# A causal convolution as banded matrices kept in DRAM, and one front part woven into a query part

## The chip, the core and the metric

The kernel runs on one core of a Trainium2 chip, as one program of about 54,000 instructions. The core has four engines that compute: TensorE (PE), VectorE (DVE), ScalarE (ACT) and GpSimd (POOL). SyncE (SP) issues most of the DMAs. Each engine works through its own instructions strictly in the order in which they were written into the program, and waits on semaphores for the others. The metric is the device time of one execution in microseconds.

## What is computed

One layer of a streaming encoder over 1024 tokens of width 1024. A shared projection feeds two groups, a convolution module and an RWKV-7 recurrence; their outputs are joined, projected, normalised, and sent through a PEER layer that picks 16 of 16,384 experts for each of 8 heads. The change touches the convolution module:

```python
u = p_conv[..., :CONV_WIDTH] * jax.nn.sigmoid(p_conv[..., CONV_WIDTH:])
u = lax.conv_general_dilated(
    u, conv_w[:, None, :], window_strides=(1,),
    padding=[(CONV_KSIZE - 1, 0)], dimension_numbers=('NWC', 'WIO', 'NWC'),
    feature_group_count=CONV_WIDTH) + conv_b
y_conv = jax.nn.silu(layer_norm(u, conv_ln_g, conv_ln_b))
...
x = layer_norm(ALPHA * x + gate1 * (jnp.concatenate([y_conv, y_rw], -1) @ w_out), ln1_g, ln1_b)
q = (adaln(x, shift2, scale2) @ peer_wq)
```

CONV_WIDTH is 512 channels and CONV_KSIZE 31 taps; each channel is convolved with its own taps over the tokens before it.

## The kernel before

The tokens are worked in two halves of 512. `inproj(h)` (from line 292) projects a half: it makes the inputs of the recurrence (r, k, v and what goes with them, stored to DRAM as AR_d, BK_d and v_d) and the gated input u of the convolution (`glu`). For half 0 this runs alone; for half 1 it is a generator whose steps are put between other work.

The recurrence is a scan over 16 chunks of 64 tokens. `solve(c)` builds and inverts a triangular system by a chain of short PE matmuls with DVE or POOL steps between them; `pass_state(c)` carries the state from chunk to chunk, and its first matmul (line 706) opens a chunk in PE's order. Solves run up to two chunks ahead. After every fourth chunk two token tiles of 128 are complete; `front(t0)` then projects 256 tokens with w_out and normalises them, and `query(t0)` multiplies them with peer_wq and sorts scores for the PEER layer. `choose` combines the sorted scores, and `gate_matrix` turns the choice into dense gate matrices, in stages of 32 tokens that are stored to G_d in DRAM. When all stages are there, the dense expert matmuls begin (lines 1294 and 1328). Three of the eight token tiles are gathered row by row instead, beside the dense part.

What sets the order: the scan's code calls `fill()` after its matmuls. Each call adds `rate[0]` to a credit; when it reaches RUN = 4, four steps of the list `side` are taken, which holds the second half's projection, then fronts and queries. Every fourth call takes one step of the list `slow`, which holds the convolution and the choices, and every twelfth one of `gates`. `RATES` gives the rate before and after chunk 3. At chunk 5 the second half's projection is finished by force, at chunk 9 the convolution, and the first entries of `firsts` (the first front and query). After the scan one loop empties the lists. A scheduler then places each instruction into its engine's order; the code's order is the priority, and it is not the final one.

`conv(h)` (from line 470) works the 512 channels as four tiles `ct` of 128 channels on partitions, 512 tokens in a row, with the 30 tokens before them in front (`ubuf`, `utail`). Of 31 taps DVE does 18, one multiply-add of 128x512 each (lines 479 and 484), in place. PE does 13 (PE_TAPS): ACT scales the identity by the tap's weights (line 490, a diagonal matrix), and PE multiplies it with the shifted window (line 492), float32 and 512 columns wide. DVE joins the two sums (line 495). Mean and variance over channels are matmuls with a matrix of ones (lines 498 and 506), and ACT, DVE and POOL finish the layer norm and the swish (lines 510 to 518), which stores conv_d for `front` to load.

A few lines say what a sentence can't:

```python
def fill():
    credit[0] += rate[0]
    fills[0] += 1
    if credit[0] >= RUN:
        credit[0] -= RUN
        for _ in range(RUN):
            step(side)
    if fills[0] % SLOW == 0:
        slow_step(1)
```

Of the kernel before, what the change touches and what calls it, by code (L numbers as in the profile page):

```python
# [10 lines left out]
F32 = mybir.dt.float32  # L11
# [22 lines left out]
HALF = 512  # L34
# [29 lines left out]
CD = 0  # L64
PIN = 3
STEPS = 4, 3
RATES = 1.0, 1.0
NPAGE = 30
TSLOW = 2
TGATE = 12  # L70
# [3 lines left out]
ABUF = 6  # L74
VBUF = 4

COLS = [("cond_b", 48), ("mu", 14), ("conv_w", 4 * KS), ("conv_b", 4), ("cln_g", 4), ("cln_b", 4),
        ("w0", 4), ("a0", 4), ("kk", 4), ("ka", 4), ("rk", 4), ("gn_g", 4), ("gn_b", 4)]
COFF = {}
_o = 0  # L80
for _n, _w in COLS:
    COFF[_n] = (_o, _o + _w)
    _o += _w
NCOLS = _o


@with_exitstack
def layer_kernel(ctx, tc, x, cols, c_row, cond_w, w_in, w2a2, g2, w_out, ln_rows, wq, keys, peer_u, peer_ut, peer_v, peer_vt, out):
# [7 lines left out]


    colt = const.tile([128, NCOLS], F32)
    ld(colt, cols)

    def col(n, i=None):
        a, b = COFF[n]
        return colt[:, a:b] if i is None else colt[:, a + i:a + i + 1]

    ident = const.tile([128, 128], F32)
# [46 lines left out]
    V.memset(ones_m, 1.0 / CW)  # L152
# [6 lines left out]
    def mm(w=512):  # L159
        return psum.tile([128, 512], F32, tag="mm", name="mm")[:, :w]  # L160
# [4 lines left out]
    def page(name, dt=F32, w=512):  # L165
        return pgp.tile([128, max(w, 512)], dt, tag="pg", name=name)[:, :w]
# [81 lines left out]
    def run(jobs):  # L248
        for j in jobs:
            yield from j  # L250

    def drain(gen):
        for _ in gen:
            pass
# [24 lines left out]
    ubuf = [fe.tile([128, 4, KS - 1 + HALF], F32, name="u", bufs=1) for _ in range(1)][0]  # L279
    utail = fe.tile([128, 4, KS - 1], F32)  # L280
    G.memset(utail, 0.0)
# [10 lines left out]
    def inproj(h, ps, pg_):  # L292
# [5 lines left out]
        def tp(name):  # L298
            return pg_.tile([128, 512], F32, tag="pg", name=name)
# [165 lines left out]

    def behind(h):
        return tc.issue_after(ready[h].ins) if h in ready else nullcontext()
    PE_TAPS = 13

    def conv(h):  # L470
        acc = []
        for ct in range(4):
            wk = lambda k: colt[:, COFF["conv_w"][0] + KS * ct + k:COFF["conv_w"][0] + KS * ct + k + 1]
            win = lambda k: ubuf[:, ct, k:k + HALF]
# [5 lines left out]
            i, j = 1, KS - PE_TAPS  # L480
            while i < KS - PE_TAPS or j < KS:
                for _ in range(3):
                    if i < KS - PE_TAPS:
                        V.scalar_tensor_tensor(a, win(i), wk(i), a, op0=OP.mult, op1=OP.add)
                        i += 1
                if j < KS:
                    n = min(2, KS - j)
                    dg = page("ctap").rearrange("p (k c) -> p k c", k=4)
                    for k in range(n):
                        A.activation(dg[:, k, :], ident, AF.Copy, scale=wk(j + k))  # L490
                    for k in range(n):
                        T.matmul(pt, dg[:, k, :], win(j + k), start=j + k == KS - PE_TAPS, stop=j + k == KS - 1)
                    j += n
                yield
            V.tensor_add(a, a, pt)
        pmn = mm()
        for ct in range(4):
            T.matmul(pmn, ones_m, acc[ct], start=ct == 0, stop=ct == 3)
        for ct in range(4):
            V.tensor_sub(acc[ct], acc[ct], pmn)  # L500
        yield
        pv = mm()
        for ct in range(4):
            s2 = page("s2")
            A.activation(s2, acc[ct], AF.Square)
            T.matmul(pv, ones_m, s2, start=ct == 0, stop=ct == 3)
        rs = page("crs")
        A.activation(rs, pv, AF.Sqrt, bias=eps_ln)
        V.reciprocal(rs, rs)
        yield  # L510
        for ct in range(4):
            y = acc[ct]
            V.tensor_mul(y, y, rs)
            A.activation(y, y, AF.Identity, bias=col("cln_b", ct), scale=col("cln_g", ct))
            sc_ = page("csig")
            A.activation(sc_, y, AF.Sigmoid)
            G.tensor_mul(y, y, sc_)
            ld(conv_d[h][ct], y)
            yield
        conv_left.remove(h)  # L520

# [267 lines left out]
    def front(t0, pg_):  # L789
# [3 lines left out]
        hp, hi = duo("ychi", F32R, pg_)  # L793
        lp, lo = duo("yclo", F32R, pg_)
        for i in range(KD // 2):
            f = pg_("ycf").rearrange("p (a t) -> p a t", a=2)
            if i < 2:
                c = t0 % HALF
                ld(f, conv_d[t0 // HALF][2 * i:2 * i + 2, :, c:c + n].rearrange("g p t -> p g t"))
# [4 lines left out]
            A.activation(hp[i], f, AF.Copy)  # L804
            G.tensor_sub(lp[i], f, hp[i].bitcast(F32))
        yield
        gate = [None, None]
        if (w_out.tensor.name, 0) not in split_d:
# [589 lines left out]
```

## Time and profile before

| what | value |
|---|---|
| median of three runs | 3205.79 us |
| lowest and highest | 3205.46 and 3208.14 us |
| the profiled execution | 3205.98 us |
| its span, first to last instruction | 3204.2 us |
| mean granted TensorE clock | 0.96 of full |
| convolution, first and last tap matmul, half 0 | 227.2 and 313.2 us from the span's start |
| first dense expert work without pause | about 1374.5 us |

Times in the profile are microseconds from the start of the span, unless marked ns. A group row gives a source line, engine, operation, the tiles written and read, and the count; then its busy time, the mean of one in ns, and the idle time of the engine ahead of it with what ended it. A float32 matmul leaves two records for each instruction. "x16" is a count of records. Matmuls overlap each other, so PE's busy time is not the sum of what each costs; the distance between neighbours is the cost of one.

### The profile page before, as it was taken

How to read it: one execution, taken by the hardware profiler on the slowest of the kernel's cores; microseconds unless marked ns; L12 is line 12 of the kernel's file. 1: busy time of each engine (PE TensorE's matmuls, PEld its weight loads, DVE VectorE, ACT ScalarE, POOL GpSimd, SP SyncE). 2: the span in 40 equal slices, each digit the busy share in tenths (PEclk: the TensorE clock that was granted, in tenths of full speed). 3: DMA queues.
4: the chain of work that ended last, by engine and by line, in shares of the span. 5: the costliest groups of instructions: out<-in, count | busy, mean ns of one | idle time of the engine just before them, and what ended most of it. 6: DMA issues, size and time to landing. Idle time of an engine off the chain costs nothing.

```text
span 3204.2 us, 53805 instructions
## 1 busy us (share of the span) xinstructions
PE 2993.7 (93%) x19952; PEld 2579.7 (81%) x19952; DVE 2513.0 (78%) x5677; ACT 1162.4 (36%) x2148; POOL 1761.6 (55%) x1368
## 2 busy tenths in 40 slices
PE   6969999899799888899999999999999999999995
PEld 4735676478678788889898898899999898999995
DVE  6379566867957899548999999988778777778788
ACT  5562444253434645643232232322223232222222
POOL 2410112143542433467777776777878778787872
PEclk9979998989789999999999999999999999999998
DMA  8876465378477998989999989899999989999994
GB/s 310 292 208 227 155 174 169 107 250 302 151 229 234 309 324 276 312 301 333 332 321 330 331 318 331 311 340 338 337 344 331 350 319 359 332 348 326 347 339 166
DMA packets 411783, 922.32 MB, mean 288 GB/s; under 512 B 81744, under 2 KB 221568, under 8 KB 389504
## 3 DMA queue, kind: packets, MB, share of 16 engines
q1 hardware_dynamic: 218688, 474.23, 43.1%
q0 software_dynamic: 110592, 402.70, 34.2%
q10 hardware_dynamic: 82240, 41.94, 4.7%
q8 instruction: 157, 2.57, 0.3%
q14 instruction: 106, 0.87, 0.1%
HBM read 788.91 MB, written 129.85 MB: 287 GB/s over the span
## 4 chain that ended last, share of the span: by engine, by line
PE 39%; DVE 12%; DMA 5%; issue 3%; POOL 1%; ACT 1%; SPq 0%; POOLq 0%; ACTq 0%; DVEq 0%
PE mg L1294 20%; PE md L1328 19%; DVE grow L1220 2%; DMA G_d<-stage 2%; DVE gy L1227 2%; DVE yacc L1333 1%; DMA grow<-peer_v,eid 1%; DMA vraw<-peer_vt 1%; POOL grow L1212 1%; DMA grow<-peer_u,eid 1%; POOL ulo L1255 1%; DVE mg L1298 0%; DVE ltkg L984 0%; DVE al L1300 0%; PE mgate L1058 0%
## 5 line engine op out<-in xcount | busy, mean ns | idle before, releaser
L1294 PE MATMUL mg<-h2h,uhi 128*128 128x320 f32 x2024 | 627.9, 310 | 12.6 <-DVE al L1300 9.5
L1294 PE MATMUL mg<-h2l,uhi 128*128 128x320 f32 x2024 | 626.3, 309 | 0.0
L1294 PE MATMUL mg<-h2h,ulo 128*128 128x320 f32 x2024 | 626.2, 310 | 0.0
L1227 DVE SCALAR_TENSOR_TENSOR gy<-grow,gz,gy 128x1024 f32<-128x1024 f32 x381 | 488.0, 1281 | 21.5 <-DMA grow<-peer_v,eid 17.3
L1328 PE MATMUL md<-vhi,al 128*128 128x512 f32 x1280 | 499.0, 391 | 0.0
L1328 PE MATMUL md<-vhi,ah 128*128 128x512 f32 x1280 | 493.1, 391 | 5.4 <-ACT ah L1299 3.8
L1328 PE MATMUL md<-vlo,ah 128*128 128x512 f32 x1280 | 497.3, 390 | 0.0
L1220 DVE SCALAR_TENSOR_TENSOR grow<-grow,gh 128x1024 f32<-128x1024 f32 x384 | 460.9, 1212 | 39.0 <-DMA grow<-peer_u,eid 35.7
L1212 POOL DMA_INDIRECT grow<-peer_u,eid x384 | 363.6, 947 | 192.3 <-DVE grow L1220 69.1
L1212 POOL DMA_INDIRECT grow<-peer_v,eid x384 | 362.8, 945 | 185.9 <-DVE gy L1227 83.8
L1294 PEld LDWEIGHTS mg<-h2h,uhi 128*128 128x128 f32 x2024 | 381.3, 188 | 21.7 <-DVE al L1300 13.3
L1294 PEld LDWEIGHTS mg<-h2l,uhi 128*128 128x128 f32 x2024 | 381.3, 188 | 4.8
L1294 PEld LDWEIGHTS mg<-h2h,ulo 128*128 128x128 f32 x2024 | 381.1, 188 | 2.8
L1255 POOL TENSOR_TENSOR ulo<-uraw,uhi 128x1024 fp32r<-128x1024 f32 x128 | 309.4, 2418 | 40.2 <-ACT uhi L1253 33.8
L1255 POOL TENSOR_TENSOR vlo<-vraw,vhi 128x1024 fp32r<-128x1024 f32 x128 | 309.3, 2416 | 24.6 <-ACT vhi L1253 20.1
L1333 DVE TENSOR_TENSOR yacc<-md,yacc 128x512 f32<-128x512 f32 x310 | 210.9, 685 | 110.9 <-PE md L1328 107.1
L1328 PEld LDWEIGHTS md<-vhi,ah 128*128 128x128 f32 x1280 | 240.1, 188 | 54.1 <-ACT ah L1299 5.3
L1054 POOL TENSOR_TENSOR ob<-mask,selt 128x384 f32<-128x384 bf16 x160 | 142.0, 899 | 256.2 <-PE mgate L1058 97.9
L1328 PEld LDWEIGHTS md<-vlo,ah 128*128 128x128 f32 x1280 | 240.6, 188 | 48.9
L1253 ACT ACTIVATE vhi<-vraw 128x1024 fp32r<-128x1024 f32 x128 | 135.2, 1056 | 398.7 <-DMA vraw<-peer_vt 369.4
L1328 PEld LDWEIGHTS md<-vhi,al 128*128 128x128 f32 x1280 | 240.5, 188 | 45.3 <-DVE al L1300 0.3
L186 POOL TENSOR_TENSOR wsplit<-wraw,wsplit 128x1024 fp32r<-128x1024 f32 x46 | 116.3, 2530 | 228.6 <-ACT wsplit L185 194.7
(405 smaller groups left out, 5764.0 us busy)
## 6 DMA issues: line engine op xcount, KB each, us to landing
uraw<-peer_ut SPq DMA_DIRECT2D x128, 512.0 KB
vraw<-peer_vt SPq DMA_DIRECT2D x128, 512.0 KB
wsplit<-split_wq SPq DMA_DIRECT2D x48, 1024.0 KB
G_d<-stage ACTq DMA_DIRECT2D x20, 2048.0 KB
gmat<-G_d SPq DMA_DIRECT2D x32, 1024.0 KB
cw<-cond_w SPq DMA_DIRECT2D x48, 512.0 KB
wsplit<-split_w_out SPq DMA_DIRECT2D x24, 1024.0 KB
split_w_in<-wsplit SPq DMA_DIRECT2D x22, 1024.0 KB
```

Source lines behind the costliest of these rows:

```text
L186: G.tensor_sub(lo, raw, hi.bitcast(F32))
L1054: G.tensor_mul(ob[:, :3], mb[:, :3], gt[:, c:c + 3, None].to_broadcast([128, 3, 128]))
L1212: G.indirect_dma_start(out=r, out_offset=None, in_=peer_u if k < 128 else peer_v, in_offset=bass.IndirectOffsetOnAxis(ap=eid[:, k % 128:k ...
L1220: V.scalar_tensor_tensor(r, r, 1.0, ht, op0=OP.mult, op1=OP.mult, accum_out=z[:, i:i + 1])
L1227: V.scalar_tensor_tensor(y, r, z[:, i - 128:i - 127], y, op0=OP.mult, op1=OP.add)
L1253: A.activation(hi, raw, AF.Copy)
L1255: G.tensor_sub(lo, raw, hi.bitcast(F32))
L1294: T.matmul(p, l[:, k, :], r[k][:, bs], start=i == 0, stop=i == 3 * KD - 1)
L1328: T.matmul(p, l[:, ts], r[:, e % 2, :], start=e == 0 and q == 0, stop=e == 3 and q == 2)
L1333: ins = V.tensor_add(ya, p, ya)
```

## The change

The convolution is laid out anew. A partition no longer holds one channel with 512 tokens in a row, but one of 32 channels and one of PH = 4 phases of the tokens (token number modulo 4). Four groups g of 32 channels fill a tile, each with 128 time steps of 4 tokens. Then one matrix of 128x128 per lag carries the taps from four phases to four phases, and LAGS = 9 lags cover 31 taps. A tile takes 4 x 9 = 36 matmuls of 128 columns, a half 144. No tap is done on DVE.

The matrices are banded: 32x32 blocks that are diagonal. For the first half POOL builds them, four to a page, as a product of a small identity (`eye32`) and the weights (line 512 of the new kernel), 36 pages in all, and stores each page to `tape_d` in DRAM (line 515). For the second half the pages are loaded back (line 510) instead. The weights come in a tile of their own, `convt`.

To bring u into phases, ACT's sigmoid and DVE's product in `glu` read PSUM with a step of four, u is stored to DRAM with four DMAs per tile, and `conv` loads it as (phase, channel) with the 8 steps before. Mean and variance use a matrix of ones in 32x32 blocks, over 16 pieces of 128 columns. The result is stored with four DMAs per tile, and `front` reads it back with two loads per page, so that ACT's and POOL's splitting steps there come in two pieces.

Beside it the order of the parts changes. At chunk 7 (MERGE) the new front, of tokens 256 to 511, is no longer put behind the first query: `beside` takes a step of each in turn, and the pair takes the query's place in `side` and in `firsts`, so that both are finished by force at chunk 9. The rate of side steps after chunk 3 falls from 1.0 to 0.5.

```diff
+MERGE = 7,
+CY = 2
+RELOAD = 1
-RATES = 1.0, 1.0
+RATES = 1.0, 0.5
+PH = 4
+LAGS = 9
...
-    conv_d = dt([4, 128, HALF], "conv_d", 2)
+    conv_d = dt([4, 128, PH, 128], "conv_d", 2)
+    tape_d = dt([LAGS, 128, 512], "tape_d", 4) if RELOAD else None
+    u_d = dt([4, PH, 32, S // PH], "u_d", 4)
...
-                s_ = tp("gsig")
-                A.activation(s_, pg, AF.Sigmoid)
-                A.activation(ubuf[:, ct, :KS - 1], utail[:, ct, :], AF.Copy)
-                V.tensor_mul(ubuf[:, ct, KS - 1:], pa, s_)
-                A.activation(utail[:, ct, :], ubuf[:, ct, HALF:], AF.Copy)
+                s_ = tp("gsig").rearrange("p (q t) -> p q t", q=PH)
+                A.activation(s_, pg.rearrange("p (t q) -> p q t", q=PH), AF.Sigmoid)
+                V.tensor_mul(s_, pa.rearrange("p (t q) -> p q t", q=PH), s_)
+                for g in range(4):
+                    ld(u_d[ct][g, :, :, 128 * h:128 * h + 128].rearrange("q c t -> c q t"), s_[32 * g:32 * g + 32])
...
+            ld(ubuf[ct][:, :, o:], u_d[ct].rearrange("g q c t -> (q c) g t")[:, :, 128 * h - LAGS + 1 + o:128 * h + 128])
+        yield
+        for ct in range(4):
             a, pt = page("cacc"), mm()
             acc.append(a)
-            with behind(0) if PIN & 1 else nullcontext():
-                V.tensor_scalar(a, win(0), wk(0), col("conv_b", ct), op0=OP.mult, op1=OP.add)
...
-                        V.scalar_tensor_tensor(a, win(i), wk(i), a, op0=OP.mult, op1=OP.add)
...
-                        A.activation(dg[:, k, :], ident, AF.Copy, scale=wk(j + k))
...
-                        T.matmul(pt, dg[:, k, :], win(j + k), start=j + k == KS - PE_TAPS, stop=j + k == KS - 1)
...
-            V.tensor_add(a, a, pt)
+            w = col("conv_w")[:, 4 * PH * LAGS * ct:4 * PH * LAGS * (ct + 1)]
+            for i in range(4 * LAGS // 4):
+                dg = page("ctap")
+                if h and RELOAD:
+                    ld(dg, tape_d[ct][i])
+                else:
+                    G.tensor_mul(dg.rearrange("p (j c) -> p j c", c=32), eye32[:, None, :].to_broadcast([128, 16, 32]),
+                                 w[:, 16 * i:16 * i + 16, None].to_broadcast([128, 16, 32]))
+                    if RELOAD:
+                        ld(tape_d[ct][i], dg)
+                for j in range(4):
+                    g, m = divmod(4 * i + j, LAGS)
+                    T.matmul(pt[:, 128 * g:128 * g + 128], dg[:, 128 * j:128 * j + 128],
+                             ubuf[ct][:, g, LAGS - 1 - m:LAGS - 1 - m + 128], start=m == 0, stop=m == LAGS - 1)
+                if i % CY == CY - 1:
+                    yield
+            V.tensor_tensor(four(a), four(pt), wide("conv_b", ct), op=OP.add)
+            yield
...
-            firsts.append(front(64 * (c - 3), page))
-            side.insert(0 if c in AHEADF else len(side), firsts[-1])
+            f_ = front(64 * (c - 3), page)
+            if c in MERGE and side:
+                m_ = beside(f_, side[-1])
+                firsts[:] = [m_ if f is side[-1] else f for f in firsts]
+                side[-1] = m_
+            elif c in AHEADF:
+                side.insert(0, f_)
+            else:
+                side.append(f_)
+            firsts.append(f_)
```

More of the change, by code (lines that the diff above doesn't have):

```diff
@@ L83 @@
     _o += _w
-NCOLS = _o
+NCOLS = COFF["conv_w"][0]
+NCONV = _o - NCOLS
 @with_exitstack
@@ L98, in layer_kernel @@
     colt = const.tile([128, NCOLS], F32)
-    ld(colt, cols)
+    ld(colt, cols[:, :NCOLS])
+    convt = []
     def col(n, i=None):
         a, b = COFF[n]
+        if a >= NCOLS:
+            a, b = a - NCOLS, b - NCOLS
+            return convt[0][:, a:b] if i is None else convt[0][:, a + i:a + i + 1]
         return colt[:, a:b] if i is None else colt[:, a + i:a + i + 1]
@@ L151, in layer_kernel @@
     ones_m = fe.tile([128, 128], F32)
-    V.memset(ones_m, 1.0 / CW)
+    V.memset(ones_m, 0.0)
+    for q in range(PH):
+        V.memset(ones_m[32 * q:32 * q + 32, 32 * q:32 * q + 32], 1.0 / CW)
+    eye32 = fe.tile([128, 32], F32, name="eye32")
+    V.tensor_reduce(eye32, ident.rearrange("p (q c) -> p c q", q=PH), axis=AX.X, op=OP.add)
     iota_q = const.tile([128, TOPK, TOPK], BF, name="iota_q")
@@ L250, in run, with beside @@
             yield from j
+    def beside(a, b):
+        a, b = [a], [b]
+        while a or b:
+            step(a)
+            step(b)
+            yield
     def drain(gen):
@@ L278, in layer_kernel @@
     V.memset(mask0.rearrange("p (c t) -> p c t", t=64)[:, :, 0:1], 0.0)
-    ubuf = [fe.tile([128, 4, KS - 1 + HALF], F32, name="u", bufs=1) for _ in range(1)][0]
-    utail = fe.tile([128, 4, KS - 1], F32)
-    G.memset(utail, 0.0)
+    ubuf = [fe.tile([128, 4, LAGS - 1 + 128], F32, name=f"u{ct}", bufs=1) for ct in range(4)]
+    for ct in range(4):
+        G.memset(ubuf[ct][:, :, 0:LAGS - 1], 0.0)
+    convt.append(fe.tile([128, NCONV], F32, name="convt"))
+    ld(convt[0], cols[:, NCOLS:])
     V.memset(last, 0.0)
@@ L467, in behind @@
         return tc.issue_after(ready[h].ins) if h in ready else nullcontext()
-    PE_TAPS = 13
     def conv(h):
+        four = lambda a: a.rearrange("p (g t) -> p g t", g=4)
+        wide = lambda n, ct: col(n)[:, 4 * ct:4 * ct + 4, None].to_broadcast([128, 4, 128])
         acc = []
         for ct in range(4):
-            wk = lambda k: colt[:, COFF["conv_w"][0] + KS * ct + k:COFF["conv_w"][0] + KS * ct + k + 1]
-            win = lambda k: ubuf[:, ct, k:k + HALF]
+            o = 0 if h else LAGS - 1
+            ld(ubuf[ct][:, :, o:], u_d[ct].rearrange("g q c t -> (q c) g t")[:, :, 128 * h - LAGS + 1 + o:128 * h + 128])
@@ L476, in conv @@
+        yield
+        for ct in range(4):
             a, pt = page("cacc"), mm()
             acc.append(a)
-            with behind(0) if PIN & 1 else nullcontext():
-                V.tensor_scalar(a, win(0), wk(0), col("conv_b", ct), op0=OP.mult, op1=OP.add)
[L480 to L494, printed above, removed]
@@ L497, in conv @@
+            V.tensor_tensor(four(a), four(pt), wide("conv_b", ct), op=OP.add)
+            yield
+        across = lambda a: a[:, None, :].to_broadcast([128, 4, 128])
+        pmn = mm(128)
+        for i in range(16):
+            T.matmul(pmn, ones_m, acc[i // 4][:, 128 * (i % 4):128 * (i % 4) + 128], start=i == 0, stop=i == 15)
         for ct in range(4):
-            T.matmul(pmn, ones_m, acc[ct], start=ct == 0, stop=ct == 3)
-        for ct in range(4):
-            V.tensor_sub(acc[ct], acc[ct], pmn)
+            V.tensor_sub(four(acc[ct]), four(acc[ct]), across(pmn))
@@ L501, in conv @@
         yield
-        pv = mm()
+        pv = mm(128)
         for ct in range(4):
@@ L505, in conv @@
             A.activation(s2, acc[ct], AF.Square)
-            T.matmul(pv, ones_m, s2, start=ct == 0, stop=ct == 3)
-        rs = page("crs")
+            for g in range(4):
+                T.matmul(pv, ones_m, s2[:, 128 * g:128 * g + 128], start=ct == g == 0, stop=ct == g == 3)
+        rs = page("crs", w=128)
         A.activation(rs, pv, AF.Sqrt, bias=eps_ln)
@@ L512, in conv @@
             y = acc[ct]
-            V.tensor_mul(y, y, rs)
-            A.activation(y, y, AF.Identity, bias=col("cln_b", ct), scale=col("cln_g", ct))
+            V.tensor_mul(four(y), four(y), across(rs))
+            for g in range(4):
+                yg = y[:, 128 * g:128 * g + 128]
+                A.activation(yg, yg, AF.Identity, bias=col("cln_b", 4 * ct + g), scale=col("cln_g", 4 * ct + g))
             sc_ = page("csig")
@@ L517, in conv @@
             G.tensor_mul(y, y, sc_)
-            ld(conv_d[h][ct], y)
+            for q in range(PH):
+                ld(conv_d[h][ct].rearrange("(g c) q t -> c q g t", c=32)[:, q], four(y)[32 * q:32 * q + 32])
             yield
@@ L795, in front @@
         for i in range(KD // 2):
-            f = pg_("ycf").rearrange("p (a t) -> p a t", a=2)
+            f, h_, l_ = pg_("ycf").rearrange("p (a t) -> p a t", a=2), hp[i], lp[i]
             if i < 2:
-                c = t0 % HALF
-                ld(f, conv_d[t0 // HALF][2 * i:2 * i + 2, :, c:c + n].rearrange("g p t -> p g t"))
+                c = t0 % HALF // PH
+                f = f.rearrange("p a (q t) -> p a q t", q=PH)
+                h_, l_ = (z.rearrange("p a (t q) -> p a q t", q=PH) for z in (h_, l_))
+                for a in range(2):
+                    ld(f[:, a], conv_d[t0 // HALF][2 * i + a, :, :, c:c + n // PH])
             else:
@@ L803, in front @@
                        rwkv_d[tile0 + t][2 * i - 4:2 * i - 2].rearrange("g p t -> p g t"))
-            A.activation(hp[i], f, AF.Copy)
-            G.tensor_sub(lp[i], f, hp[i].bitcast(F32))
+            for a in range(2) if i < 2 else (slice(0, 2),):
+                A.activation(h_[:, a], f[:, a], AF.Copy)
+                G.tensor_sub(l_[:, a], f[:, a], h_[:, a].bitcast(F32))
         yield
```

21 lines of the change are left out of this document (9 added, 12 removed).

## The prediction

> **What bounds the kernel now.** I read the head of the page first, then the busy time of each engine by stage, then the groups of instructions, then the chain of waits.
>
> ```profile
> span 3204.2 us, 53805 instructions
> PE 2993.7 (93%) x19952; PEld 2579.7 (81%) x19952; DVE 2513.0 (78%) x5677; ACT 1162.4 (36%) x2148; POOL 1761.6 (55%) x1368
> ```
>
> The profiled execution took 3205.98 us, its span is 3204.2, and the median of the runs is 3205.79. I add to and take from 3206.0. A PE that is busy for 93% is an average over stages, so here are the stages. The columns are the stretch, its length, then PE, PE weight load, DVE, ACT and POOL busy with instruction counts, the granted clock, DMA share and GB/s.
>
> ```profile
> 0.00:213.00 213.00, 163.42 (x631) 117.66 (x631) 110.77 (x221) 119.29 (x207) 63.62 (x37) 0.90 0.80 277
> 213.00:254.50 41.50, 35.20 (x107) 19.48 (x104) 37.77 (x81) 16.28 (x40) 2.53 (x2) 0.92 0.77 217
> 254.50:368.50 114.00, 104.75 (x767) 67.40 (x766) 94.73 (x192) 41.56 (x99) 8.12 (x7) 0.91 0.59 197
> 368.50:534.50 166.00, 162.93 (x1655) 118.50 (x1653) 93.73 (x180) 72.89 (x134) 19.04 (x14) 0.98 0.54 157
> 534.50:665.50 131.00, 117.95 (x901) 72.35 (x899) 109.32 (x164) 52.10 (x116) 42.27 (x21) 0.91 0.48 159
> 665.50:827.50 162.00, 153.13 (x1768) 131.05 (x1764) 114.36 (x515) 62.41 (x130) 62.24 (x35) 0.92 0.83 286
> 827.50:999.50 172.00, 150.72 (x1627) 124.31 (x1628) 125.87 (x342) 75.18 (x158) 80.20 (x84) 0.81 0.57 182
> 999.50:1327.00 327.50, 287.60 (x2292) 273.15 (x2292) 285.99 (x1251) 170.00 (x350) 114.56 (x118) 0.97 0.88 297
> 1374.50:3204.20 1829.70, 1777.19 (x9939) 1617.14 (x9937) 1516.31 (x2684) 516.25 (x850) 1344.77 (x1024) 0.99 0.90 326
> ```
>
> I put the borders where the first state matmul of a chunk of the scan starts. Of that matmul's line alone, the same view counts 16 records for each chunk, which shows which chunks lie in a stage: 0 from 254.5, 1 to 4, 5 and 6, and 7 to 10 from 665.5.
>
> ```profile
> 254.50:368.50 114.00, 1.00 (x16) 0.72 (x16) 0.91 0.59 197
> 534.50:665.50 131.00, 1.34 (x32) 1.09 (x32) 0.91 0.48 159
> 665.50:827.50 162.00, 2.90 (x64) 2.27 (x64) 0.92 0.83 286
> ```
>
> The last stretch, the dense experts, is 1829.7 us with PE busy for 97%. The change adds and removes nothing there, so I carry it over unchanged. All that can move lies before 1374.5. Two stages there have DVE nearly full with the convolution, and these are its groups (busy us, mean ns):
>
> ```profile
> L484 DVE SCALAR_TENSOR_TENSOR cacc<-u,colt,cacc 128x512 f32<-128x512 f32 x136 | 109.7, 834 | 0.3
> L492 PE MATMUL mm<-u,ctap 128*128 128x512 f32 x208 | 101.0, 627 | 0.2 <-DVE xt L827 0.2
> L490 ACT ACTIVATE ctap<-ident,colt 128x128 f32<-128x128 f32 x104 | 33.7, 390 | 20.4 <-PE mm L492 16.8 <-DVE fa L581 2.3 <-DVE ia L575 1.0
> L495 DVE TENSOR_TENSOR cacc<-cacc,mm 128x512 f32<-128x512 f32 x8 | 5.4, 679 | 0.8 <-PE mm L492 0.8
> ```
>
> By the stage view of that DVE line alone, 14.1 + 35.5 = 49.6 us of the 109.7 lie in 213 to 368.5, and 60.1 in 534.5 to 665.5:
>
> ```profile
> 213.00:254.50 41.50, 14.09 (x20) 0.92 0.77 217
> 254.50:368.50 114.00, 35.53 (x49) 0.91 0.59 197
> 534.50:665.50 131.00, 60.09 (x68) 0.91 0.48 159
> ```
>
> So from 213 to 368.5 DVE works 132.5 of 155.5 us, and the scan's short matmuls, whose results DVE must mask and copy, stand in line behind taps.
>
> **The change, part by part.** PE first. A tap over 512 columns is two records; one of 128 columns also, and the gate matrices are such matmuls already.
>
> ```profile
> 264.09 2.84 PE L492 MATMUL mm<-u,ctap 128*128 128x512 f32 x6
> 886.88 1.06 PE L1058 MATMUL mgate<-oa,ob 128*128 128x128 f32 x8
> ```
>
> Taking one record's own 0.63 us off, six old ones come every (2.84 - 0.63) / 5 = 0.44 us; 52 matmuls of one half are 104 x 0.44 = 46 us. Eight narrow ones come every (1.06 - 0.29) / 7 = 0.11 us (0.29 is the mean of that line); the new half has 144 matmuls, 288 x 0.11 = 32 us. PE saves 14 us per half. The column means count as many columns as before. DVE loses 68 taps per half and keeps one addition per tile at L495's price. ACT loses 52 tap copies.
>
> POOL gets 36 tape products of 128x512 in the first half. No row has both inputs broadcast; the nearest of that shape are these:
>
> ```profile
> L517 POOL TENSOR_TENSOR cacc<-cacc,csig 128x512 f32<-128x512 f32 x8 | 10.7, 1357 | 24.0 <-ACT csig L516 24.0
> L430 POOL TENSOR_TENSOR a<-a,nr 128x512 f32<-128x512 f32 x8 | 12.6, 1572 | 139.9 <-DVE nr L425 96.0 <-issue 27.1 <-DVE rstd L216 16.8
> L1054 POOL TENSOR_TENSOR ob<-mask,selt 128x384 f32<-128x384 bf16 x160 | 142.0, 899 | 256.2 <-PE mgate L1058 97.9 <-DVE mask L1047 85.2 <-ACT oa L1053 43.7
> ```
>
> I take 1.36; the low end is 0.90 x 512/384 = 1.20, the high end 1.57, and twice the first for an access pattern that no row shows. POOL's order before, at the start of the scan (a, xm and MT are POOL's products of the mixing and of the solve):
>
> ```order
> L442 TENSOR_TENSOR xm<-xm,W 128x512
> L430 TENSOR_TENSOR a<-a,nr 128x512
> L442 TENSOR_TENSOR xm<-xm,W 128x512
> L640 TENSOR_TENSOR MT<-MT,eye_1458 128x256 x3
> L517 TENSOR_TENSOR cacc<-cacc,csig 128x512 x4
> ```
>
> and now:
>
> ```order
> L468 TENSOR_TENSOR xm<-xm,W 128x512
> L512 TENSOR_TENSOR ctap<-eye_168,convt 128x512 x9
> L456 TENSOR_TENSOR a<-a,nr 128x512
> L468 TENSOR_TENSOR xm<-xm,W 128x512
> L512 TENSOR_TENSOR ctap<-eye_168,convt 128x512 x20
> L673 TENSOR_TENSOR MT<-MT,eye_1487 128x256
> L512 TENSOR_TENSOR ctap<-eye_168,convt 128x512 x7
> L673 TENSOR_TENSOR MT<-MT,eye_1487 128x256 x2
> ```
>
> Twenty-nine tapes now stand ahead of the first solve's MT, and 36 ahead of the second's. PE, in the same place (arl is the scan's input, u the convolution's):
>
> ```order
> L518 MATMUL mm<-u_187,ctap 128x128 x5
> L665 MATMUL bank_1480<-arl,bkl 128x128 x4
> L518 MATMUL mm<-u_187,ctap 128x128 x14
> L665 MATMUL bank_1480<-arl,bkl 128x128 x4
> L518 MATMUL mm<-u_187,ctap 128x128 x9
> L739 MATMUL bank_1479<-SN,arl 64x64 x6
> ```
>
> So chunk 0's matmuls wait for 27 tapes, and POOL is the new pace-maker. It is free from 209.11 + 1.27 = 210.4 (first row below), so the last tape is there at 210.4 + 36 x 1.36 + 2 x 1.4 = 262. Before, PE issued its last tap at 313.2 (second row).
>
> ```profile
> 209.11 1.27 POOL L442 TENSOR_TENSOR xm<-xm,W 128x512 f32<-128x512 f32 x1 [2.86 <-DVE sq L438]
> L492 PE MATMUL mm<-u,ctap x104: 590/592/1220, 227.2 to 313.2; 128*128 128x512 f32 x104
> L620 SPq DMA_DIRECT2D arl<-AR_d x16: 359/377/939, 232.6 to 850.4; - x16
> 260.21 0.39 PE L198 MATMUL mm<-hlo,wsplit 128*128 128x512 f32 x1
> 260.44 0.62 PE L198 MATMUL mm<-hhi,wsplit 128*128 128x512 f32 x2
> ```
>
> Behind the last tap 55 us passed until chunk 1. That part now holds 28 more input matmuls, 6 us at 0.23 each (two in a row take 0.62, one 0.39, in the last two rows), so chunk 1 comes at 262 + 3 + 61 = 326 instead of 369: 43 us. SP's queue takes three off: the 36 tape stores and the u transfers stand ahead of loads that the scan needs, each with 0.38 us to issue (the third row); the loads of chunk 0, at 232.6 before, wait for tape 18 at 238. **First half: -40**, between -55 (1.20, no stall) and 0 (double price).
>
> Second half, 534.5 to 665.5: DVE falls from 109 to about 50 us and PE from 118 to 104, and both stop being full together. The tapes come back by 36 loads of 256 KB, 9.4 MB, 33 us at the 286 GB/s that the next stage reaches; DMA was busy for 0.48 x 131 = 63 us, so 96 in all fit beside PE's 104. PE then decides: 105 us. **Second half: -26**, between -35 and 0 (loads that stand behind the wraw waits in SP's order).
>
> The merge and the rate. In the stage of chunks 7 to 10 the same 384 query and 96 front matmuls are issued as before, but later: PE's order behind chunk 8's first state matmuls was
>
> ```order
> L706 MATMUL bank_1450<-SN,arl 64x64 x8
> L198 MATMUL mm<-h2hi,wsplit 128x256 x2
> L198 MATMUL mm<-h2lo,wsplit 128x256
> L198 MATMUL mm<-h2hi,wsplit 128x256 x2
> L198 MATMUL mm<-h2lo,wsplit 128x256
> ```
>
> and is now
>
> ```order
> L739 MATMUL bank_1479<-SN,arl 64x64 x8
> L678 MATMUL bank_1480<-eye_1487,vl 64x64
> L679 MATMUL bank_1480<-eye_1487,vl 64x64
> L678 MATMUL bank_1480<-eye_1487,vl 64x64
> L679 MATMUL bank_1480<-eye_1487,vl 64x64
> ```
>
> Chunks 7 and 8 run bare, and query and front crowd into 9 and 10. A chunk cost no less than 31 us even where PE was not full:
>
> ```profile
> 902.00:933.50 31.50, 1.39 (x16) 1.01 (x16) 0.84 0.83 265
> 968.50:999.20 30.70, 0.68 (x16) 0.54 (x16) 0.91 0.80 252
> ```
>
> Then 32 MB (16 raw tiles of 0.5 MB, 16 stores of 1 MB, 8 reloads of 1 MB) at 286 / 0.83 = 345 GB/s take 93 us, 115 at 277 GB/s. 62 + 110 - 162 = **+10**, between -7 and +30.
>
> After the scan 584 instead of 520 gate matmuls remain, but 984 instead of 1056 of the query. Sixteen more groups of four cost DVE a mask and a product each, 0.68 + 0.28 us, 15 us; 6 fewer score matmuls mean 6 fewer sorts of five steps like L784's, 0.28 x 5 x 6 = 8 us less. DVE is busy for 286 of 327.5 us there: **+7**, 0 to 20.
>
> ```profile
> L1047 DVE TENSOR_TENSOR mask<-iota_b,selbank 128x1024 bf16<-128x1024 bf16 x128 | 86.1, 678 | 19.8 <-POOL ob L1054 11.0 <-ACT oa L1053 6.0 <-ACT selt L1027 1.6
> L1055 DVE TENSOR_TENSOR ob<-mask,selbank 128x128 f32<-128x128 bf16 x128 | 33.5, 279 | 35.4 <-PE mgate L1058 30.3 <-POOL ob L1054 2.4
> L784 DVE FIND_INDEX8 vi<-vi,s 128x8 uint32<-128x128 f32 x96 | 26.6, 284 | 0.0
> ```
>
> Before 213, 16 u stores and ACT and DVE reading every fourth column: **+2**, 0 to 8 (16 issues at 0.38 us, if nothing hides them).
>
> The sum: 3206 - 40 - 26 + 10 + 7 + 2 = **3159 us**.
>
> [...]
>
> **The rivals.**
>
> *POOL's tapes cost double.* With 2.7 us each the last is there at 311, as late as the last tap was: the first term is gone, 3199. For it: POOL's rows scatter, and no row has two broadcasts. Against: L1054 broadcasts one input at no visible cost.
>
> *Half the clock in the bare chunks.* Eight gate matmul records took 2.07 us in a stretch with PE idle, 1.06 later:
>
> ```profile
> 862.83 2.07 PE L1058 MATMUL mgate<-oa,ob 128*128 128x128 f32 x8
> ```
>
> If chunks 7 and 8, whose PE work by the order is about 20 us, run so, they take 20 us more: 3179. Against: a chunk waits mostly for DVE. [...]
>
> *The gate stages end the front, and begin later: slower.* The chain of waits passes through the stores of the gate stages:
>
> ```profile
> 1340.71 15.39 DMA G_d<-stage
> L1066 ACTq DMA_DIRECT2D G_d<-stage x20: 366/366/400, 902.5 to 1375.5; - x20
> ```
>
> Nineteen steps took 473 us. The first stage stood behind chunk 11 in PE's order, now behind chunk 14. With my terms chunk 15 begins at 999 - 54 = 945 and the first stage ends near 925, against 902.5. If the steps keep their 24.9 us, the dense part starts 22 us later, whatever was saved: 3228. It decides if a stage can't come faster than that; but the last ones came 10 to 15 us apart, since the store above was the wait.
>
> *Nothing lost in the merge.* Without the third and fourth term, and with the first two at -48 and -33: 3127.
>
> **How the numbers follow.** Forecast 0.57, double tapes 0.12, half clock 0.13, gate stages 0.10, nothing lost 0.08. The range from 3120 to 3199 leaves out the gate stages, half the double tapes and little of the edges, about 2 in 10. A measurement here can tell 0.2%, 6.4 us, from no change. Faster: 0.55 of the forecast, 0.13, 0.08 and half of the tapes, 0.07, sum 0.83; same 0.07; slower 0.10.
>
> **What would show it.** Chunk 1's first state matmul near 328, the tapes' mean at 1.2 to 1.6 us, chunk 7's near 602, chunk 11's near 774, chunk 15's near 945, dense from about 1328. The forecast is wrong if the tapes are dearer, if tape loads arrive after PE wants them, if chunks 9 and 10 take over 130 us, or if the dense part isn't 1830 us long.

## The result and the profile after

The changed kernel takes 3174.0 us (median of four runs, 3168.5 to 3174.9) against 3205.6 of the kernel before: a ratio of 0.990, with a 95% interval from 0.9877 to 0.9922, so 25 to 39 us faster. A second series gave 3173.1 us and 0.9906 (0.9888 to 0.9925). The profiled execution took 3173.26 us, 32.7 less than the one of before.

The head of the page of the changed kernel:

```profile
span 3171.5 us, 54882 instructions
PE 2968.4 (94%) x20416; PEld 2622.4 (83%) x20416; DVE 2415.8 (76%) x5538; ACT 1133.7 (36%) x2058; POOL 1809.2 (57%) x1415
```

DVE lost 97 us of work and POOL gained 48, PE's busy time fell by 25. Now the stages, with the columns of the prediction's table (length, PE, weight load, DVE, ACT, POOL, clock, DMA share, GB/s). The borders are again the first state matmuls of chunks, here of 0, 1, 2, 5, 7, 11 and 15.

```profile
213.00:265.70 52.70, 49.67 (x316) 42.88 (x314) 39.62 (x82) 14.76 (x28) 36.05 (x31) 0.96 0.88 277
265.70:339.20 73.50, 72.18 (x788) 59.14 (x787) 46.00 (x93) 29.43 (x68) 17.61 (x15) 0.98 0.83 289
339.20:396.80 57.60, 53.86 (x471) 37.19 (x471) 41.89 (x83) 22.54 (x42) 4.23 (x3) 0.88 0.73 238
396.80:521.00 124.20, 119.13 (x1244) 88.35 (x1242) 67.39 (x126) 51.57 (x94) 16.03 (x13) 0.96 0.57 162
521.00:625.00 104.00, 99.10 (x1070) 86.25 (x1068) 44.81 (x83) 36.89 (x70) 34.44 (x20) 0.95 0.80 278
625.00:801.00 176.00, 158.56 (x1790) 138.65 (x1786) 100.15 (x396) 66.92 (x137) 59.83 (x36) 0.83 0.79 270
801.00:957.50 156.50, 136.41 (x1527) 116.32 (x1527) 133.28 (x502) 60.87 (x135) 71.66 (x73) 0.84 0.60 198
```

Chunk 1 to chunk 2, the third row, is 57.6 us long (58.4 by the two starts). Before it was 42.5 with PE never idle:

```profile
368.50:411.00 42.50, 42.50 (x435) 30.13 (x434) 24.67 (x46) 18.79 (x37) 4.59 (x3) 1.00 0.59 172
```

In the ledger below, "mark" is the hundredth matmul record of the line that opens the dense part (L1294 before, L1331 now), a clearer border than the first record. All of it is read off the starts of those records, in us; "second profile" is another profile of the changed kernel (after_again below).

| stretch | before | after | difference | second profile | forecast |
|---|---|---|---|---|---|
| 213 to chunk 2 | 198.5 | 183.9 | -14.6 | -17.2 | -40 |
| chunks 2 to 4 | 123.8 | 123.7 | -0.1 | -1.7 | 0 |
| chunks 5, 6 | 130.5 | 104.0 | -26.5 | -26.6 | -26 |
| chunks 7 to 10 | 162.1 | 176.4 | +14.3 | +13.5 | +10 |
| chunk 11 to the mark | 561.2 | 555.6 | -5.6 | -12.2 | +7 |
| behind the mark | 1815.1 | 1814.9 | -0.2 | +0.4 | 0 |

Two profiles of the same kernel lie up to 12 us apart at the mark (1356.6 and 1344.9), but only 3 at chunk 2. So I read causes from the stages, and a whole time only from its interval.

One row is 25 us short of its forecast, the first half's. The page's own chain of waits names a suspect that stands in no term of the prediction, a DMA of `cond_w`:

```profile
PE mg L1331 22%; PE md L1365 21%; PE mm L214 5%; PE mm L860 2%; PE mgate L1095 2%; DMA cw<-cond_w 2%; DVE grow L1257 2%; DVE gy L1264 2%; PE mm L518 1%; DVE mask L1084 1%; DVE yacc L1370 1%; DMA G_d<-stage 1%; PE bank L697 1%; PE bank L723 1%; POOL grow L1249 1%
```

These are the columns of the modulation that come from the condition vector: `cond_some` loads a 512 KB tile and DVE multiplies it with the vector and sums. 16 of 48 are done at the start, 32 beside the scan's first chunks. They share two buffers with the raw weights (WRAW = 2). By tile, the changed kernel and then the kernel before:

```profile
L291 SPq DMA_DIRECT2D cw<-cond_w x48: 327/328/1687, 8.8 to 361.7; - x48
L293 DVE SCALAR_TENSOR_TENSOR cw<-cw,silc x48: 1182/1224/3427, 17.5 to 370.1; 128x1024 f32<-128x1024 f32 x48
  DMA cw<-cond_w: 21.8, 18
```

```profile
L267 SPq DMA_DIRECT2D cw<-cond_w x48: 327/328/990, 8.3 to 329.3; - x48
L269 DVE SCALAR_TENSOR_TENSOR cw<-cw,silc x48: 1211/1218/3395, 17.6 to 333.6; 128x1024 f32<-128x1024 f32 x48
  DMA cw<-cond_w: 4.8, 10
```

The last line of each is DVE's idle time until such a load (us, times). The products are the same, but DVE waits 21.8 us instead of 4.8, and the last product starts at 370, well behind chunk 1 (339), where before it started at 334, ahead of chunk 1 (369). Between chunk 1 and chunk 2 alone, the stage view of this tile counts 22 records of DVE, 11 products with their read-outs, 13.6 us of work, and the waits there for its loads are 12.7 us; before, none of the products lay in this stretch:

```profile
338.50:396.90 58.40, 13.55 (x22) 0.88 0.74 239
DVE cw L293 <- DMA cw<-cond_w: 12.7, 9, 5.3
```

### The profile page after: what moved, and what is told of

It reads as the page before. It is cut to its first block, busy times and chain, and to the rows that moved or that the text cites. A ratio compares the mean times of both kernels' runs of the same rounds, so it can differ in the third digit from the quotient of the medians.

```text
span 3171.5 us, 54882 instructions
## 1 busy us (share of the span) xinstructions
PE 2968.4 (94%) x20416; PEld 2622.4 (83%) x20416; DVE 2415.8 (76%) x5538; ACT 1133.7 (36%) x2058; POOL 1809.2 (57%) x1415
## 4 chain that ended last, share of the span: by engine, by line
PE 59%; DVE 19%; DMA 6%; issue 4%; POOL 2%; ACT 2%; SPq 0%; POOLq 0%; ACTq 0%; DVEq 0%
PE mg L1331 22%; PE md L1365 21%; PE mm L214 5%; PE mm L860 2%; PE mgate L1095 2%; DMA cw<-cond_w 2%; DVE grow L1257 2%; DVE gy L1264 2%; PE mm L518 1%; DVE mask L1084 1%; DVE yacc L1370 1%; DMA G_d<-stage 1%; PE bank L697 1%; PE bank L723 1%; POOL grow L1249 1%
## 5 line engine op out<-in xcount | busy, mean ns | idle before, releaser
L1331 PE MATMUL mg<-h2h,uhi 128*128 128x320 f32 x2024 | 626.9, 310 | 7.8 <-DVE al L1337 7.7
L1331 PE MATMUL mg<-h2l,uhi 128*128 128x320 f32 x2024 | 625.8, 309 | 0.0
L1331 PE MATMUL mg<-h2h,ulo 128*128 128x320 f32 x2024 | 625.4, 309 | 0.0
L1331 PEld LDWEIGHTS mg<-h2h,uhi 128*128 128x128 f32 x2024 | 380.5, 188 | 16.9 <-DVE al L1337 12.0
L1331 PEld LDWEIGHTS mg<-h2l,uhi 128*128 128x128 f32 x2024 | 380.4, 188 | 5.3
L1331 PEld LDWEIGHTS mg<-h2h,ulo 128*128 128x128 f32 x2024 | 380.3, 188 | 2.8
L214 PE MATMUL mm<-hhi,wsplit 128*128 128x512 f32 x672 | 227.6, 412 | 8.7 <-ACT gsig L389 5.4
```

Of the source, the lines that this page charges most:

```text
L214: T.matmul(pt, l[:, k, :], r[k], start=i == 0, stop=i == 3 * KD - 1)
L1331: T.matmul(p, l[:, k, :], r[k][:, bs], start=i == 0, stop=i == 3 * KD - 1)
```

## The experiments

**The theories.** T: the taps were the cover of this chain. With two buffers a tile can't be loaded before the one two places ahead has been multiplied; while it was on its way DVE had taps to do. Without taps DVE stands at the product, in order, and the solves' steps stand behind the wait and the products. S: the 36 tape stores, on SP's queue and as holders of POOL's pages, ate the gain. A: the merge and the slower rate ate it.

The start of the first state matmul of some chunks, in us, and the mark, for all that was profiled:

| kernel | 0 | 1 | 2 | 5 | 7 | 11 | 15 | mark |
|---|---|---|---|---|---|---|---|---|
| before | 255 | 369 | 411 | 535 | 666 | 828 | 999 | 1389 |
| after | 266 | 339 | 397 | 521 | 625 | 801 | 957 | 1357 |
| after_again | 268 | 341 | 394 | 516 | 620 | 796 | 950 | 1345 |
| conv_only | 268 | 340 | 395 | 518 | 623 | 788 | 977 | 1369 |
| no_rate | 266 | 339 | 394 | 516 | 621 | 785 | 975 | 1373 |
| rebuild | 251 | 356 | 404 | 521 | 629 | 809 | 960 | 1368 |
| wraw4 | 268 | 341 | 382 | 511 | 612 | 797 | 959 | 1350 |
| before_wraw4 | 258 | 382 | 422 | 553 | 694 | 864 | 1010 | 1409 |
| after_nocond | 264 | 339 | 378 | 509 | 615 | 792 | 939 | 1336 |
| late_tapes | 249 | 354 | 396 | 522 | 623 | 808 | 955 | 1347 |
| wraw4_act | 278 | 349 | 391 | 520 | 625 | 812 | 973 | 1365 |
| conv_wraw4 | 267 | 340 | 380 | 511 | 610 | 799 | 964 | 1337 |
| conv_wraw4_b | 267 | 339 | 380 | 508 | 608 | 792 | 954 | 1328 |
| conv_wraw4_late | 249 | 357 | 395 | 526 | 636 | 811 | 972 | 1345 |

Each edit also lets the scheduler place other instructions anew, so a row differs by more than its edit.

**1. The parts of the change.** First the convolution without merge and rate, then with the merge alone.

```diff
-MERGE = 7,
+MERGE = ()
-RATES = 1.0, 0.5
+RATES = 1.0, 1.0
```

> The changed kernel with MERGE empty and RATES back to 1.0, 1.0: the convolution's part alone. Read off the two traces, that part brought chunk 2 forward by 14.5 us and the stage of chunks 5 and 6 by 27 us, and the stage of chunks 7 to 10 became 14 us longer. Theory A (the merge and the slower rate cost what they were priced at, 10 + 7 us): stage of chunks 7 to 10 back at 162 us, the dense part begins some 10 to 17 us earlier than with the whole change, time 3157 to 3165 us. Rival B (that stage is longer because everything ahead of it came earlier, so its 32 MB of transfers decide, whatever the order): stage at 170 to 176 us, time 3170 to 3178. Rival C (merge and rate pay later, by taking gate work out of the scan): time 3180 or more.

```diff
-RATES = 1.0, 0.5
+RATES = 1.0, 1.0
```

> The changed kernel with RATES back to 1.0, 1.0 and the merge kept. Theory A (the slow rate leaves chunks 8 and 9 bare, at a granted clock of 0.65 and 0.50, and crowds 10 and 11): the clock between chunk 7 and chunk 9 comes back over 0.8, the stage of chunks 7 to 10 falls from 176 to some 162 us, time 3160 to 3167. Rival B (transfers decide that stage): stage within 4 us of 176, time 3170 to 3178.

> The changed kernel itself once more, beside the others on one chip. The whole change against the convolution alone (3181.8 us, 0.9914): theory C (merge and slower rate together repay some 8 us after the scan): 0.9885 to 0.9900, chunk starts within 4 us of the first profile. Rival A (they cost 10 us or more, and the first measurement was a lucky chip): 0.993 or more.

Measured: conv_only 3181.8 us, 0.9914 (0.9897 to 0.9930); no_rate 3185.2, 0.9933 (0.9915 to 0.9951); the whole change once more 0.9906 (0.9888 to 0.9925), its profile within 3 us of the first up to chunk 2, and 12 ahead at the mark. A falls as the cause: without merge and rate the time is not shorter. For conv_only that is what rival C forecast; no_rate came out longer than either theory had it, and after_again between its two. In its stage A was right about the length: chunks 7 to 10 take 165 us in conv_only and 164 in no_rate, and 176 with the slower rate (the clock between chunk 7 and chunk 9 did not come back over 0.8 in no_rate, it was 0.76). But conv_only needs 580 us from chunk 11 to the mark, the whole change 556 and 549. Merge and rate together are worth 0.0008 to 0.0015 of the time, which these intervals can't tell from nothing; the slow rate by itself, 0.9933 against 0.9906 and 0.9899, gains 9 to 11 us by the ratios, with intervals that overlap. What the convolution brings is nearly all of the result.

**2. Tapes built twice, none stored.**

```diff
-RELOAD = 1
+RELOAD = 0
```

> The changed kernel with RELOAD = 0: no tape is stored or loaded, POOL builds all 36 again in the second half. Theory S (the tape stores held the first half up: POOL waited 8.0 us for them, and SP's queue carries 36 of them): chunk 0's first state matmul at 257 instead of 265.7, chunk 2's at 386 to 389 instead of 397, the second half's stage at 104 to 108 us since POOL has room for 38 us more there, time 3162 to 3168. Rival T (what is missing in the first half is the chain of condition products, each waiting for its load): chunk 0 some 8 us earlier, but chunk 2 at 395 to 397, time 3172 to 3178. Rival U (the second half's gain needs the loads): its stage at 115 us or more, time over 3180.

Measured: 3185.0 us, 0.9928 (0.9916 to 0.9941). S's forecast failed: two of chunk 0's 16 matmuls started at 251, the rest at 269, and chunks 1 and 2 came later than with the stores (356 and 404). DVE's waits for condition tiles were 28.2 us there. The last tape of the first half ended at 279 us, against 277 with the stores, so doing without the stores did not bring the tapes earlier; why chunk 1 was 18 us later all the same stays open. The second half needs no loads: 629 - 521 = 108 us, against 104. T's number for chunk 2 (395 to 397) and its time (3172 to 3178) were missed too.

**3. Four buffers for the condition's tiles**, in the changed kernel and in the kernel before.

```diff
-WRAW = 2
+WRAW = 4
```

> The changed kernel with four buffers instead of two for the raw weights, which the 32 condition products between chunks 0 and 2 share. Theory T (with the taps gone nothing covers the load of each condition tile; DVE waited 21.8 us for them, SP 26 us for DVE to free a buffer): DVE's waits on these loads fall under 6 us, chunk 2's first state matmul comes at 382 to 388 instead of 397, time 3159 to 3166. Rival S (the tape stores are what holds the first half up): waits fall too, but chunk 2 stays at 394 to 397, time 3170 to 3176.

> The kernel before with four raw buffers instead of two. Theory T (before, DVE's taps covered the loads of the condition tiles: DVE waited 4.8 us for them in all): chunk 2's first state matmul within 4 us of 411.5, time within 5 us of the kernel before, ratio 0.998 to 1.002. Rival G (four buffers help any version of this kernel, through the projections' raw weights): 10 us or more faster, ratio under 0.997, seen before 213 us or in chunks 7 to 10.

Measured: wraw4 3161.5 us, 0.9858 (0.9843 to 0.9874); before_wraw4 3218.8, 1.0049 (1.0030 to 1.0067). DVE's waits for condition tiles in wraw4, by the tile view:

```profile
  DMA cw<-cond_w: 10.0, 4
```

and the stretch from chunk 1 to chunk 2 there, by the stage view, then what is left of this chain in it (records of the tile on DVE, and the waits for its loads):

```profile
341.00:382.00 41.00, 40.40 (x452) 29.27 (x450) 29.58 (x54) 17.22 (x36) 4.60 (x3) 1.00 0.80 268
340.80:381.80 41.00, 4.89 (x8) 1.00 0.80 268
DVE cw L293 <- DMA cw<-cond_w: 5.1, 1, 5.1
```

Chunk 2 came at 382, 15 us earlier, as T said; PE is full there again, and the clock is 1.00 instead of 0.88. DVE's wait fell to 10.0 us in all, not under 6. In the stretch itself two things shrank together, the waits from 12.7 to 5.1 us and the products from 11 to 4, since the others now came ahead of chunk 1. In the kernel before, the same edit costs 13 us, where T forecast no change and rival G a gain: both missed. Its last condition product came at 307 instead of 334, its last tap matmul at 342 instead of 313, and chunk 1 at 382 instead of 369. DVE was busy for 117 of the 129 us from 213 to 342 there; I read it so that faster loads let the products, 32 x 1.22 = 39 us, go ahead of taps, but no run tests that. So four buffers are no help in themselves; they help where the cover is gone.

**4. The condition's chain taken out.** Another order of instructions could still have been what helped in wraw4. This kernel leaves out the loads and products of 32 columns and sets these to 0.5; it computes something else, and only its times are read.

```diff
-                cond_some(range(16 + 4 * ct, 20 + 4 * ct))
+                V.memset(mod[:, 16 + 4 * ct:20 + 4 * ct], 0.5)
-                    cond_some(range(32 + 4 * ct, 36 + 4 * ct))
+                    V.memset(mod[:, 32 + 4 * ct:36 + 4 * ct], 0.5)
```

> The changed kernel with 32 of the 48 columns of the condition's modulation left out (set to a constant): 32 loads of 512 KB and 32 DVE products of 1.22 us are gone from the stretch of chunks 0 to 2. Theory T (that chain of loads and products is what held chunk 2 back): chunk 2's state matmul at 374 to 384 instead of 394 to 397, as with four buffers or earlier, time 3150 to 3163. Rival R (the gain with four buffers came from another order of the instructions, not from the waits): chunk 2 at 390 or later, time 3168 or more.

Measured: 3150.6 us, 0.9837 (0.9819 to 0.9855). Chunk 2 at 378, and chunk 1 to 2:

```profile
339.00:378.00 39.00, 39.00 (x418) 27.73 (x418) 21.34 (x40) 14.98 (x29) 3.27 (x3) 1.00 0.42 137
```

With two buffers and no chain PE is never idle there. So the chain is what held the stretch from chunk 1 to chunk 2, as T said. How much of the 15 us is the waits and how much the products' own time is not separated: the edit takes both away, and wraw4 lessens both. The chain is also late from its beginning: the fifth of the 32 products starts at 265 in the changed kernel and at 245 before, and no run takes that part of its lateness by itself. Chunk 1 itself stayed at 339: the chain does not hold that one.

**5. Tapes that begin later.** In the changed kernel chunk 0 comes 11 us later than before, at 266. Two things stand in its trace. The first is on DVE, at the end of half 0's mixing (start, duration, engine, line), the changed kernel:

```profile
216.05 1.27 DVE L453 TENSOR_SCALAR sq<-a,colt 128x512 f32<-128x512 f32 x1
217.24 2.06 DVE L439 TENSOR_TENSOR_SCAN cum<-mask,sig 128x512 f32<-128x512 f32 x1
219.23 1.47 DVE L454 SCALAR_TENSOR_TENSOR sq<-sq,xm 128x512 f32<-128x512 f32 x1
220.62 1.26 DVE L448 TENSOR_SCALAR nr<-nr 128x512 f32<-128x512 f32 x1
...
233.73 0.69 DVE L467 TENSOR_TENSOR sq<-m,xm 128x512 f32<-128x512 f32 x1 [0.61 <-PE m L466]
```

and in the same kernel POOL's tapes (seven from 212.4 to 221.6), and SP's queue, where tape stores stand ahead of the loads of chunk 0 (L653), which went out at 232.6 to 238 before:

```profile
212.37 9.23 POOL L512 TENSOR_TENSOR ctap<-eye,convt 128x512 f32<-128x512 f32 x7 [0.76 <-DVE hlo L252]
...
234.76 2.62 SPq L515 DMA_DIRECT2D tape_d<-ctap  x3
...
242.40 3.84 SPq L515 DMA_DIRECT2D tape_d<-ctap  x4
246.57 0.38 SPq L653 DMA_DIRECT2D arl<-AR_d  x1
```

The edit makes the tapes read a copy of `eye32` that DVE writes only after the mixing:

```diff
+        eyeb = page("eyeb", w=32)
+        with behind(0):
+            V.tensor_copy(eyeb, eye32)
...
-                    G.tensor_mul(dg.rearrange("p (j c) -> p j c", c=32), eye32[:, None, :].to_broadcast([128, 16, 32]),
+                    G.tensor_mul(dg.rearrange("p (j c) -> p j c", c=32), eyeb[:, None, :].to_broadcast([128, 16, 32]),
```

> The changed kernel with a copy of the small identity that DVE makes only after the last product of half 0's mixing; the tapes read that copy, so POOL builds none before some 230 us. In the changed kernel's trace DVE's steps of the last mixing that began during a tape took 2.06 instead of 1.22, 1.47 instead of 0.67 and 1.26 instead of 0.42 us. Theory P (POOL's tapes hold those DVE steps up, which delays the end of the mixing by 6 us and the start of the scan with it): these steps take 1.22, 0.67 and 0.42 again, DVE's last product of the mixing comes at 228 instead of 233.7, chunk 0's scores matmuls at 250 to 253 instead of 258, chunk 0's state matmul at 256 to 262; the tapes, 36 in 40 to 46 us, end at 272 to 280, so chunk 1 comes at 335 to 340 and the time stays at 3168 to 3175. Rival (the delay comes from the stores in SP's queue alone): the steps keep their longer times, or chunk 0's scores stay at 257 or later.

Measured: 3163.9 us, 0.9881 (0.9864 to 0.9898), an interval that overlaps those of the whole change. The same DVE steps:

```profile
215.10 0.48 DVE L453 TENSOR_SCALAR sq<-a,colt 128x512 f32<-128x512 f32 x1
215.49 1.22 DVE L439 TENSOR_TENSOR_SCAN cum<-mask,sig 128x512 f32<-128x512 f32 x1
216.62 0.67 DVE L454 SCALAR_TENSOR_TENSOR sq<-sq,xm 128x512 f32<-128x512 f32 x1
217.21 0.43 DVE L448 TENSOR_SCALAR nr<-nr 128x512 f32<-128x512 f32 x1
...
229.13 0.69 DVE L467 TENSOR_TENSOR sq<-m,xm 128x512 f32<-128x512 f32 x1 [2.17 <-PE m L466]
```

P holds for the steps: 4.6 us earlier at the last of them, and chunk 0 at 249, better than forecast. But the last tape ended at 296, not by 280, chunk 1 came at 354, and chunk 2 at 396, where it was; the time was a little better than forecast. The start of chunk 0 was not what the end of the half waits for. The last tape is nearer to it: in every version but one, chunk 1 came 52 to 66 us after the last tape's end (in rebuild 77).

**6. The stores on ACT's queue**, beside four buffers.

```diff
-                        ld(tape_d[ct][i], dg)
+                        A.dma_start(tape_d[ct][i], dg)
```

> Four raw buffers, and the 36 tape stores issued by ACT instead of SP. Theory Q (the stores in SP's queue hold up the loads of chunk 0, which came at 251 to 260 us with them and at 242 to 250 without, against 233 to 238 before the change): chunk 0's scores matmuls at 258 instead of 264, chunk 1's state matmul 4 to 7 us earlier than 341, time 3154 to 3158. Rival (the delay of chunk 0 comes from the tapes that stand ahead of the mixing's products on POOL, not from the stores, and ACT now waits for tapes): chunk 1 at 340 to 345, time 3160 to 3166.

Measured: 3179.1 us, 0.9918 (0.9901 to 0.9936), 18 us worse than wraw4, and past the rival's end too. Q falls: the scores of chunk 0 started at 273. PE waited 10.6 us for tapes, 5.4 in wraw4.

**7. The convolution alone with four buffers**, once more, and with the late tapes.

> The convolution's part alone (no merge, rates 1.0, 1.0) with four raw buffers. Theory T: the same 12 us as the buffers gave with merge and rate, so 3181.8 - 12 = 3170, chunk 2 at 382 to 386. If they only help where merge and rate are (transfers of the query's weights in chunks 9 and 10): 3178 to 3184.

> The convolution's part alone with four raw buffers once more, beside its late-tapes sister on one chip: 0.9800 to 0.9850 of the kernel before if 3153 us was no accident; 0.987 or more if it was.

> The convolution's part alone, four raw buffers, and the late tapes: a try at the best version. If the earlier start of the scan holds: chunk 0 at 256 to 262, time 3146 to 3152. If the tapes then come too late for PE: 3153 to 3162.

Measured: conv_wraw4 3153.4 us, 0.9824 (0.9799 to 0.9849), and 3146.5, 0.9817 (0.9800 to 0.9834): the fastest version, 52 to 59 us faster than before. With the late tapes 3163.9, 0.9874 (0.9859 to 0.9889): worse, and past both forecasts. T's 12 us were too few: conv_wraw4 is 28 us better than conv_only, 15 of them at chunk 2. The rest lies behind chunk 7: from there to the mark conv_only takes 745 us, conv_wraw4 727 and 720, the kernel before 723. And with four buffers the merge and the rate cost something: 0.9858 (0.9843 to 0.9874) against 0.9824 and 0.9817, 11 to 13 us, the second interval (0.9800 to 0.9834) apart from it. The first interval (0.9799 to 0.9849) still overlaps it. What conv_only loses behind chunk 7 stays open; a trace with the waits of the query's weights there, chunk by chunk, would be the next step.

## Why the prediction was right, and where it was not

The forecast was 3159 us with a range from 3120 to 3199, the measurement 3174: the right direction and inside the range, with two thirds of the forecast's gain (32 of 47 us). That the sum is off by no more than 14 us is partly luck: the first half alone missed by 25, and 13 came back from chunk 11 to the mark, for a reason that was not in the sum. The chunks came later than the signs that were named: chunk 7 at 625 instead of 602, chunk 11 at 801 instead of 774, chunk 15 at 957 instead of 945.

*First half, -40: too much by 25 us.* Two steps of that term failed. The larger is one that the sum takes without saying: chunk 1 earlier by 43 less 3 us was entered as a gain of the whole, as if everything after it would be earlier by as much. Chunk 1 did come 30 us earlier (339), but 16 of them were given back before chunk 2. I had counted DVE's lost taps as a gain only, and not named what they hid. The condition's loads have two buffers and a wait of 4.8 us before; without taps 21.8, and 11 of the products fell behind chunk 1. Taking the chain out (chunk 2 at 378) or giving it two more buffers (382) returns those 15 us; this was shown. The remaining 11 us or so are in chunk 1 itself, 339 against the 326 to 328 that I worked out. The price of a tape was on the safe side, 1.05 us by the median instead of 1.36:

```profile
L512 POOL TENSOR_TENSOR ctap<-eye,convt x36: 1041/1051/2034, 212.4 to 276.2; 128x512 f32<-128x512 f32 x36
  DMA tape_d<-ctap: 8.0, 6
```

But the last came at 277, not 262: POOL did not start at 210.4 but at 212.4, the mixing's and the solve's products stand between, some tapes took up to 2.03 us (the rows sum to 44 us, not 36 x 1.05 = 38), which I put down to collisions with DVE (the two from 235.0 us took 2.02 each beside its condition products, the five from 239.0, with DVE idle, 1.05), and eight us went by until a stored page was free. My sum took the 36 as one unbroken run. From the last tape's end to chunk 1 it was 61 us, and 64 were forecast (3 + 61). The edge of -55 does not follow from the terms: with 1.20 us a tape and no stall they give -49.

*Second half, -26: right.* 104.0 us against 105. PE is busy for 99 of 104, DVE for 45, and the DMA share rose from 0.48 to 0.80, as the tape loads made it (0.47 in rebuild, which has none). Rebuilding instead of loading gave 108, so the loads are not needed for this term.

*Merge and rate, +10 and +7: the first near, in part by luck, the second of the wrong sign.* Chunks 7 to 10 took 14 us more, with chunks 7 and 8 bare at a low clock, as in the rival:

```profile
625.00:655.00 30.00, 24.51 (x349) 20.66 (x346) 21.25 (x74) 15.43 (x36) 10.25 (x10) 0.65 0.73 225
655.00:673.00 18.00, 13.63 (x196) 11.47 (x196) 6.14 (x16) 7.31 (x19) 3.82 (x3) 0.50 0.50 139
```

They took 30 and 18 us all the same, 48 together where 71.5 were spent before, with little for PE to do (545 records, 826 before), and the 20 us of the rival did not come. Chunks 9 and 10 then took 128 us where the sum has 110, a value between its 93 and 115 for which it gives no step; 14 us too many in the one pair and 18 too few in the other nearly cancel. From chunk 15 to the mark it was +10 and +5, as priced. What I missed lies between chunks 11 and 15, which the sum passes over: that stretch shrank by 16 us. The 128 gate records that went behind chunk 15 are missing there (112 instead of 240), so I had entered the work where it arrives and not where it left. But they do not set its length alone: with the old rate it took 190 us at 160 such records (no_rate) and 188 at 240 (conv_only), against 172 at 240 in the kernel before. Why it shrank stays open. The runs with and without merge and rate show what the two cost in all, where 17 us were forecast: nothing that can be told from zero with two buffers, 11 to 13 us with four.

*Gate stages that end the front:* this rival did not come. The first gate store was issued at 929.2 instead of 902.5, 27 us later, and the last at 1348.4 instead of 1375.5, 27 us earlier: 419 us for nineteen steps where it was 473.

*Doubled tapes:* no, as above. *Before 213, +2:* POOL's product of the mixing at 209.1 came at 210.3. *Dense part:* the same to 0.2 us.

## What to carry to other kernels

When an engine is relieved, ask what its work was covering: list the loads with few buffers whose consumer stands in order on that engine, and price each as if nothing ran beside it. A part that is moved has two entries, where it arrives and where it leaves, and both belong in the sum. And a buffer count that suits one bound is wrong after the bound has moved: four buffers took 12 to 28 us off the new kernel and cost the old one 13.

## What the hardware showed that was not expected

POOL and DVE got in each other's way. On POOL's side, tapes beside DVE's condition products took 2.02 us instead of 1.05. Four DVE steps that began during a tape took longer by about 0.8 us, where a tape beside an idle DVE took 1.05: 2.06 instead of 1.22 us for the scan, 1.47 instead of 0.67, 1.26 instead of 0.42, 1.27 instead of 0.48; in late_tapes, with the tapes moved away, they took 1.22, 0.67, 0.43 and 0.48. L467, which reads PSUM, kept its time (0.69 us beside a tape and without). The prediction's sum for the tapes had left this out.

The granted clock differed between two profiles of one kernel in the same stretch. In the first profile of the changed kernel it was 0.73 for 25 us ahead of chunk 2:

```profile
372.00:397.00 25.00, 23.57 (x205) 16.38 (x206) 16.63 (x34) 11.79 (x21) 4.23 (x3) 0.73 0.70 205
```

In the second it was 0.97 over the whole stretch from 340 to 397 us, where the first had 0.88, and chunk 1 to chunk 2 took 53 us instead of 57.6. By the starts of chunks 1 and 2 it was 53.4 and 58.4 us, against 42.5 before. So with the clock near full 11 of the 16 us were still lost; the other 5 go with the lower clock, though nothing here shows which of the two made the other.
